# Half of the conditioning blocks of a scan stage computed by GpSimd, VectorE and one matmul instead of eight matmuls

## The chip, the cores and the metric

The kernel runs on one NeuronCore of a Trainium2 chip. TensorE multiplies matrices, VectorE, ScalarE and GpSimd work on rows of 128 partitions, and SyncE issues most of the transfers between HBM and the on-chip memory. The metric is the device time of one execution in microseconds (µs); lower is better. In the rows below PE is TensorE (PEld its weight loads), DVE is VectorE, ACT is ScalarE, POOL is GpSimd and SPq is SyncE's queue.

## The reference, cut to what matters

The model is one layer over 1024 tokens of width 1024. A conditioning vector `c` gives six rows of 1024 numbers; rows 3 and 4 shift and scale the input of the second half of the layer.

```python
sc = jax.nn.silu(c)
mod = (sc @ ada_w[i] + ada_b[i]).reshape(-1, 6, D_MODEL)
x, ctx = mixer_sublayer(x, ctx, mod, ...)            # projection, two-way scan, output projection
x = x + mod[:, 5, None, :] * peer(modulate(rms_norm(x, norm2_w[i]), mod[:, 3], mod[:, 4]), ...)
return rms_norm(x, final_norm_w)
```

## The kernel before, in words

The program is laid out by hand: every engine runs its instructions in the order in which the Python code records them, and an instruction that waits holds up all that stands behind it on the same engine. Of the whole span the change touches the scan of the mixer, from about 353 to 527 µs.

The scan has two loops over blocks of 128 tokens. The first loop (called backward here, `pre` in the code) has twelve turns; the last eight of them carry a state from block 7 down to block 0. A usual turn on TensorE is: transposes (`natural`, L596 and L600), one key product (`key_products`, L361), the carried state's product (`carried`, L644), the new state (`state`, L615) and the decay (`reach`, L634). The state passes through VectorE: `state` ends in L622 and L624, and the next turn's L644 needs the tile `h` that L624 writes. GpSimd scales the tokens (`weigh`, L607, tile `xw`, needed by L615 of the next turn; and L603) and, for the second loop, spreads step sizes over a block (`spread`, L653, tiles `pf` and `pb`, 1024 elements in each partition). The second loop (forward) goes from block 0 to 7; its turn is longer, with sixteen products of `decays` (L698 and L699, which read `pf` and `pb`) and up to four key products.

Beside the scan run two other jobs. `key_products` multiplies a weight with a key in two steps, stores the result (`m_dram<-h2T`, L365) and loads the next pair (L347, L348); after its last store it loads the eight parts of `w_out` into the same tiles (L369). The other job is `modulation`: 24 blocks `ld` of `ada_w`, of 8x128 columns (512 KB) each, loaded into two buffers by `ask` (L294). Blocks 0 to 7 give a gate and are weighted on GpSimd (L316), added up on VectorE (L318 to L321) and summed by a matmul. Blocks 8 to 23 give the columns for shift and scale, each by eight matmuls of one column (L334, fp32, so that each is recorded twice). `beside`, at the end of each turn, lets the generators in `later` go on; `ask` stands just ahead of it and issues loads while fewer than two blocks are in `ready`. After the scan the loop over `later` drains what is left, four small VectorE operations (L337 to L340) form `b2c` and `s2c`, and the output projection begins with `gated(0)` on VectorE (L793).

Of the kernel before, what the change touches and what calls it, by code (L numbers as in the profile page):

```python
# [8 lines left out]
F32 = mybir.dt.float32  # L9
# [5 lines left out]
OP = mybir.AluOpType  # L15
# [3 lines left out]
P = 128  # L19
D = 1024  # L20
KD = D // P
# [51 lines left out]
def layer_kernel(ctx, tc, A, dbg=None):  # L73
    nc = tc.nc
# [10 lines left out]
    ones = glob.tile([P, P], F32, name="ones")  # L85
# [21 lines left out]
    sc = glob.tile([P, KD, 2], F32, name="sc")  # L107
# [27 lines left out]
    lpr = bc_st.enter_context(tc.tile_pool(name="lpr", bufs=2))  # L135
# [132 lines left out]
    queue, later, spare, call = [], [], [0.0], [0]  # L268

    def beside(us):  # L270

        spare[0] += us
        call[0] += 1
        for run in (queue, later):
            for g in list(run):
                while spare[0] > 0:
                    t = next(g, None)
                    if t is None:
                        run.remove(g)
                        break  # L280
                    if t < 0:
                        break
                    spare[0] -= t
        spare[0] = min(spare[0], 0.0)

    ready, since, asked = {}, {}, [0]

    def ask():

        while asked[0] < 24 and len(ready) < 2:  # L290
            j = asked[0]
            ready[j] = lpr.tile([P, KD, P], F32, name="ld")
            since[j] = call[0]
            nc.sync.dma_start(ready[j], ada[:, :, 2048 + j * P:2048 + (j + 1) * P])  # L294
            asked[0] += 1

    def modulation():

        nc.sync.dma_start(gater, A["ada_b"][2048:3072].partition_broadcast(P))
        last = []  # L300

        def spread(j, wa):
            pr = prs[:, j % 4]
            nc.tensor.matmul(pr, ones, wa, start=True, stop=True)
            g = gater[:, j * P:(j + 1) * P]
            nc.vector.tensor_tensor(g, pr, g, op=OP.add)

        prs = psL.tile([P, 4, P], F32, name="pc")
        for j in range(KD):
            while j not in ready:  # L310
                yield -1
            while last and last[0][0] < call[0]:
                spread(*last.pop(0)[1:])
                yield 0.25
            w = ready[j]
            nc.gpsimd.tensor_tensor(w, w, sc[:, :, 0:1].to_broadcast([P, KD, P]), op=OP.mult)  # L316
            yield -1
            nc.vector.tensor_tensor(w[:, :4], w[:, :4], w[:, 4:], op=OP.add)  # L318
            nc.vector.tensor_tensor(w[:, :2], w[:, :2], w[:, 2:4], op=OP.add)
            wa = lpr.tile([P, P], F32, name="wa", bufs=3)  # L320
            nc.vector.tensor_tensor(wa, w[:, 0], w[:, 1], op=OP.add)  # L321
            del ready[j]
            last.append((call[0], j, wa))
            yield 1.1
        yield -1
        while last:
            spread(*last.pop(0)[1:])

        for j in range(KD, 3 * KD):
            while j not in ready or call[0] < since[j] + 2:  # L330
                yield -1
            w = ready.pop(j)
            for k in range(KD):
                nc.tensor.matmul(prs[:, 0, j:j + 1], w[:, k], sc[:, k, 0:1], start=k == 0, stop=k == KD - 1)  # L334
            yield 0.1
        yield -1
        nc.vector.tensor_tensor(b2c, prs[:, 0, KD:2 * KD], adab[:, 24:32], op=OP.add)  # L337
        nc.vector.tensor_tensor(s2c, prs[:, 0, 2 * KD:3 * KD], adab[:, 32:40], op=OP.add)
        nc.vector.tensor_scalar(s2c, s2c, 1.0, None, op0=OP.add)
        nc.vector.tensor_tensor(s2c, s2c, n2c, op=OP.mult)  # L340
        yield 1.0

    def key_products():

        def load(g):
            sk = s2p.tile([P, P], F32, name="sk")
            nc.sync.dma_start(h2T[:, g % KD], A["wqT"][g * P:(g + 1) * P, :])  # L347
            nc.sync.dma_start(sk, A["skT"][g])  # L348
            return h2T[:, g % KD], sk

        nxt = load(0)
        yield
        for g in range(16):
            wq, sk = nxt
            if g + 1 < 16:
                nxt = load(g + 1)
            for k4 in range(2):
                pm = psK.tile([P, 4, P], F32, name="pk")
                for a in range(4):
                    k = k4 * 4 + a  # L360
                    nc.tensor.matmul(pm[:, a], wq[:, k * P:(k + 1) * P], sk, start=True, stop=True)  # L361
                ms = wq.rearrange("p (k n) -> p k n", n=P)[:, k4 * 4:k4 * 4 + 4]
                nc.scalar.activation(ms, pm, AF.Copy)
                if k4:
                    nc.sync.dma_start(m_dram.rearrange("(k p) n -> p k n", p=P)[:, :, g * P:(g + 1) * P],  # L365
                                      wq.rearrange("p (k n) -> p k n", n=P))
                yield
        for k in (4, 5, 6, 7, 0, 1, 2, 3):
            nc.sync.dma_start(h2T[:, k], A["w_out"][k * P:(k + 1) * P, :])  # L369


    with ExitStack() as st:
# [123 lines left out]

        held = {}
        later.append(modulation())
        for n, c in enumerate(order):

# [80 lines left out]
    with ExitStack() as st:  # L581
# [149 lines left out]
        for z in range(NT):  # L731
# [19 lines left out]
            step_keys(1)  # L751
            ask()
            beside(2.2)
        for q in later:
            for _ in q:
                call[0] += 1
                ask()

        for _ in keys:
            pass  # L760
# [483 lines left out]
    with ExitStack() as st:  # L1244
# [85 lines left out]
        more, self_end = [], object()  # L1330
# [300 lines left out]
```

## Time and profile before

| | |
|---|---|
| median of 3 runs | 3053.84 µs (3052.66 to 3054.78) |
| the profiled execution, its own time | 3052.06 µs |
| its span | 3050.3 µs |
| TensorE busy in the span | 93% |
| mean granted TensorE clock | 0.968 |
| TensorE busy from 480 to 500 µs, in the forward loop | 20.00 of 20.00 µs |

The span is what the trace covers; the execution's own time has 1.76 µs around it. The median of the runs lies 1.78 µs over the profiled execution, and sums made in the trace are carried over to the median as differences. The clock is given as a share of full speed: 1.00 is 2.4 GHz and 0.50 is 1.2 GHz.

### The profile page before, as it was taken

The numbers are of one execution on the slowest core, as the hardware profiler recorded it, in microseconds if no ns is written. First come the engines' busy times: TensorE is split into PE (matmuls) and PEld (weight loads), VectorE is DVE, ScalarE is ACT, GpSimd is POOL, SyncE is SP. The second block draws the span as 40 slices with busy tenths as digits, with TensorE's granted clock in tenths as the row PEclk, the third lists the DMA queues.
The fourth block names the chain that finished last, engine by engine and source line by source line (L and its number), as shares of the span: only waits on it lengthen the run. The fifth ranks groups of instructions, "written<-read, shape, count | busy, mean of one in ns | idle before, by whom it ended". The sixth has DMA issues, their size and how long they took to land.

```text
span 3050.3 us, 41960 instructions
## 1 busy us (share of the span) xinstructions
PE 2836.3 (93%) x15129; PEld 2391.2 (78%) x15129; DVE 2570.6 (84%) x5084; ACT 1060.9 (35%) x2026; POOL 1326.0 (43%) x1043
## 2 busy tenths in 40 slices
PE   7999899998888876999999999999999999999996
PEld 3777698764555556898888998998998898998995
DVE  4898756659999999889989998888998888888886
ACT  3224333333667664332222222222222322322222
POOL 0212343420000002666566656566666566666650
PEclk8999899999999987999999999999999999999998
DMA  6211256250221235888889999998998998999993
GB/s 214 61 36 42 86 165 213 77 189 15 118 107 63 111 125 192 308 312 301 311 297 361 324 346 343 326 340 320 337 344 317 334 357 318 336 342 318 328 326 119
DMA packets 334545, 722.68 MB, mean 237 GB/s; under 512 B 24560, under 2 KB 167168, under 8 KB 333056
## 3 DMA queue, kind: packets, MB, share of 16 engines
q0 software_dynamic: 112176, 408.47, 37.1%
q1 hardware_dynamic: 222160, 311.53, 29.5%
q8 instruction: 119, 1.95, 0.2%
q14 instruction: 90, 0.74, 0.1%
HBM read 658.56 MB, written 61.35 MB: 236 GB/s over the span
## 4 chain that ended last, share of the span: by engine, by line
PE 58%; DVE 27%; issue 5%; DMA 5%; POOL 3%; ACT 2%; SPq 0%; DVEq 0%; POOLq 0%; ACTq 0%
PE pa L996 22%; PE pv L1444 8%; PE pv L1445 8%; PE pv L1443 8%; PE pa L68 4%; DVE o L1219 3%; DVE cfm L413 2%; DVE oh L1091 2%; DVE ob L1211 2%; POOL gr L1286 2%; DVE oh L1089 2%; DVE gr L1311 1%; DVE ef L1077 1%; PE pq L953 1%; PE po L68 1%
## 5 line engine op out<-in xcount | busy, mean ns | idle before, releaser
L1286 POOL DMA_INDIRECT gr<-in_peer_v_dram,idx x384 | 546.8, 1424 | 309.3 <-DVE h2T L1323 209.7
L1286 POOL DMA_INDIRECT gr<-in_peer_u_dram,idx x384 | 524.1, 1365 | 361.4 <-DVE gr L1311 249.2
L1444 PE MATMUL pv<-vl,wh 128*128 128x512 f32 x1240 | 495.5, 400 | 19.5 <-DVE vl L61 17.3
L1323 DVE SCALAR_TENSOR_TENSOR h2T<-gr,wv,h2T 128x1024 f32<-128x1024 f32 x381 | 488.5, 1282 | 13.6 <-DMA gr<-in_peer_v_dram,idx 6.0
L1443 PE MATMUL pv<-vh,wl 128*128 128x512 f32 x1240 | 493.4, 398 | 1.5 <-ACT vh L60 1.4
L1445 PE MATMUL pv<-vh,wh 128*128 128x512 f32 x1240 | 493.6, 398 | 0.0
L1311 DVE SCALAR_TENSOR_TENSOR gr<-gr,h2T 128x1024 f32<-128x1024 f32 x384 | 455.5, 1220 | 23.5 <-DMA gr<-in_peer_u_dram,idx 23.3
L60 ACT ACTIVATE vh<-v 128x512 fp32r<-128x512 f32 x256 | 161.5, 632 | 656.1 <-PE pv L1445 616.7
L996 PE MATMUL pa<-hh,ul 128*128 128x320 f32 x2000 | 335.0, 310 | 3.2 <-DVE ul L988 3.2
L996 PE MATMUL pa<-hh,uh 128*128 128x320 f32 x2000 | 334.6, 309 | 0.0
L996 PE MATMUL pa<-hl,uh 128*128 128x320 f32 x2000 | 334.0, 309 | 0.3 <-ACT ga L1406 0.3
L996 PEld LDWEIGHTS pa<-hl,uh 128*128 128x128 f32 x2000 | 304.8, 188 | 3.3 <-ACT ga L1406 0.6
L996 PEld LDWEIGHTS pa<-hh,ul 128*128 128x128 f32 x2000 | 304.2, 188 | 3.7 <-DVE ul L988 3.7
L996 PEld LDWEIGHTS pa<-hh,uh 128*128 128x128 f32 x2000 | 304.4, 188 | 0.0
L1444 PEld LDWEIGHTS pv<-vl,wh 128*128 128x128 f32 x1240 | 235.0, 190 | 80.0 <-DVE vl L61 22.8
L1406 ACT ACTIVATE ga<-pa 128x320 f32<-128x320 f32 x252 | 109.2, 436 | 525.2 <-PE pa L996 507.1
L1443 PEld LDWEIGHTS pv<-vh,wl 128*128 128x128 f32 x1240 | 235.1, 190 | 57.8 <-ACT vh L60 2.4
L61 DVE TENSOR_TENSOR vl<-v,vh 128x512 fp32r<-128x512 f32 x256 | 176.4, 690 | 122.5 <-ACT vh L60 114.9
L1445 PEld LDWEIGHTS pv<-vh,wh 128*128 128x128 f32 x1240 | 235.3, 190 | 56.1
L1197 PEld LDWEIGHTS pg<-o,o 128*128 128x128 f32 x1280 | 174.1, 207 | 128.2 <-ACT o L1214 109.2
L1197 PE MATMUL pg<-o,o 128*128 128x128 f32 x1280 | 188.0, 297 | 75.7 <-ACT o L1214 67.3
L1214 ACT ACTIVATE o<-ob,tr 128x128 f32<-128x128 bf16 x640 | 209.4, 399 | 96.4 <-DVE ob L1211 94.4
(344 smaller groups left out, 4241.5 us busy)
## 6 DMA issues: line engine op xcount, KB each, us to landing
v<-in_peer_v_dram SPq DMA_DIRECT2D x256, 256.0 KB
u<-in_peer_ut_dram SPq DMA_DIRECT2D x87, 512.0 KB
g_dram<-stg SPq DMA_DIRECT2D x10, 4096.0 KB
gm<-g_dram SPq DMA_DIRECT2D x64, 640.0 KB
h2T<-in_peer_ut_dram SPq DMA_DIRECT2D x41, 512.0 KB
ld<-in_ada_w_dram SPq DMA_DIRECT2D x24, 512.0 KB
w<-in_w_in_t_dram SPq DMA_DIRECT2D x21, 512.0 KB
raw<-in_ada_w_dram SPq DMA_DIRECT2D x8, 1024.0 KB
```

Of the source, the lines that this page charges most:

```text
L60: nc.scalar.activation(hi, src, AF.Copy)
L61: (eng or nc.vector).tensor_tensor(lo, src, hi.bitcast(F32), op=OP.subtract)
L68: nc.tensor.matmul(out, a(k)[i], b(k)[j], start=start and t == 0 and k == 0, stop=stop and t == 2 and k == n - 1)
L996: nc.tensor.matmul(pa[half], x[:, k], y[:, k, half * TH:half * TH + TH], start=t == 0 and k == 0, stop=t == 2 and k == KD - 1)
L1197: nc.tensor.matmul(pg[:, j], o2[:, j], o1[:, j], start=True, stop=True)
L1214: nc.scalar.activation(o2[:, j], ob[:, :, j], AF.Copy, scale=tr[:, 1, t4 * 4 + j:t4 * 4 + j + 1])
L1286: nc.gpsimd.indirect_dma_start(out=g, out_offset=None, in_=A[t], in_offset=bass.IndirectOffsetOnAxis(ap=idx[:, b, e:e + 1], axis=0))
L1311: nc.vector.scalar_tensor_tensor(g, g, 1.0, h2, op0=OP.mult, op1=OP.mult, accum_out=act[:, e:e + 1])
L1323: nc.vector.scalar_tensor_tensor(ac, g, wv[:, e:e + 1], ac, op0=OP.mult, op1=OP.add)
L1443: nc.tensor.matmul(Out.pv[t], wl[:, sl], self.vh, start=i == 0, stop=False)
L1444: nc.tensor.matmul(Out.pv[t], wh[:, sl], self.vl, start=False, stop=False)
L1445: nc.tensor.matmul(Out.pv[t], wh[:, sl], self.vh, start=False, stop=i == GE - 1)
```

## The change

Of blocks 8 to 23 the even ones (8, 10, ... 22) still go through eight matmuls. The odd ones (9, 11, ... 23) go to a new generator, `other_columns`: GpSimd multiplies the block by the conditioning vector, VectorE adds its eight slices in three operations, and one matmul with a column of ones sums over the partitions. That matmul is recorded when the next odd block has been given to GpSimd. A block is given to GpSimd as soon as its load has been asked for. The drain after the scan now steps both generators in turn.

```diff
-        for j in range(KD, 3 * KD):
+        later.append(other_columns(prs))
+        for j in range(KD, 3 * KD, 2):
             while j not in ready or call[0] < since[j] + 2:
                 yield -1
             w = ready.pop(j)
             for k in range(KD):
                 nc.tensor.matmul(prs[:, 0, j:j + 1], w[:, k], sc[:, k, 0:1], start=k == 0, stop=k == KD - 1)
             yield 0.1
-        yield -1
+        while len(later) > 1:
+            yield -1
...
+    def other_columns(prs):
+
+        wa = None
+        for j in range(KD + 1, 3 * KD + 2, 2):
+            while j < 3 * KD and j not in ready:
+                yield -1
+            if j < 3 * KD:
+                w = ready[j]
+                nc.gpsimd.tensor_tensor(w, w, sc[:, :, 0:1].to_broadcast([P, KD, P]), op=OP.mult)
+            if wa is not None:
+                nc.tensor.matmul(prs[:, 0, j - 2:j - 1], wa, ones[:, 0:1], start=True, stop=True)
+            yield -1
+            if j < 3 * KD:
+                nc.vector.tensor_tensor(w[:, :4], w[:, :4], w[:, 4:], op=OP.add)
+                nc.vector.tensor_tensor(w[:, :2], w[:, :2], w[:, 2:4], op=OP.add)
+                wa = lpr.tile([P, P], F32, name="wa", bufs=3)
+                nc.vector.tensor_tensor(wa, w[:, 0], w[:, 1], op=OP.add)
+                del ready[j]
+                yield 1.1
...
-        for q in later:
-            for _ in q:
-                call[0] += 1
-                ask()
+        while later:
+            for q in list(later):
+                if next(q, self_end) is self_end:
+                    later.remove(q)
+            call[0] += 1
+            ask()
```

Lines behind the new code stand 22 further down in the changed kernel (24 behind the drain): L361 is L383, L365 is L387, L653 is L675.

The first place is SyncE's queue in the backward loop, before the change: one load of a block (`ld`) to each turn, one of them right behind a store of the key products and one in the turn between.

```order
L365 DMA m_dram<-h2T 128x8x128
L294 DMA ld<-in_ada_w_dram 128x8x128
L347 DMA h2T<-in_wqT_dram 128x1024
L348 DMA sk<-in_skT_dram 128x128
L294 DMA ld<-in_ada_w_dram 128x8x128
L365 DMA m_dram<-h2T 128x8x128
L294 DMA ld<-in_ada_w_dram 128x8x128
```

The same queue with the change, from blocks 11 and 12 on.

```order
L387 DMA m_dram<-h2T 128x8x128
L294 DMA ld<-in_ada_w_dram 128x8x128 x2
L369 DMA h2T<-in_wqT_dram 128x1024
L370 DMA sk<-in_skT_dram 128x128
L387 DMA m_dram<-h2T 128x8x128
L294 DMA ld<-in_ada_w_dram 128x8x128 x2
```

Two loads, the odd block's first, now stand together behind every store, in every other turn; both buffers come free at the end of the turn ahead. In the forward loop they stand together once in two turns.

The second place is TensorE in two turns of the backward loop, before the change: each turn ends in eight matmuls.

```order
L615 MATMUL ps<-xw,bn_2342 128x256 x2
L634 MATMUL psg<-tri,dtx 128x128 x4
L334 MATMUL pc<-sc,ld 128x1 x8
L596 MATMUL pdg<-ident,xsT 128x128 x4
L600 MATMUL pcb<-ident,BT 128x128 x2
L361 MATMUL pk<-sk,h2T 128x128 x4
L644 MATMUL ps<-CT,h_2432 128x128 x4
L615 MATMUL ps<-xw,bn_2401 128x256 x2
L634 MATMUL psg<-tri,dtx 128x128 x4
L334 MATMUL pc<-sc,ld 128x1 x8
```

The same two turns with the change.

```order
L637 MATMUL ps<-xw,bn_2335 128x256 x2
L656 MATMUL psg<-tri,dtx 128x128 x4
L355 MATMUL pc<-ones,wa 128x1
L618 MATMUL pdg<-ident,xsT 128x128 x4
L622 MATMUL pcb<-ident,BT 128x128 x2
L383 MATMUL pk<-sk,h2T 128x128 x4
L666 MATMUL ps<-CT,h_2427 128x128 x4
L637 MATMUL ps<-xw,bn_2396 128x256 x2
L656 MATMUL psg<-tri,dtx 128x128 x4
L335 MATMUL pc<-sc,ld 128x1 x8
```

A turn that ends in one matmul (L355, for the odd block loaded two turns ahead) now alternates with one that ends in eight (L335, for the even block whose load was issued in the turn ahead of it). Until the last store of the key products, thirteen groups of eight become seven groups and five single matmuls.

The third place is GpSimd in the forward loop with the change; before it, the same rows stood there without L353.

```order
L629 TENSOR_TENSOR xw<-xn_2623,wgt 128x512
L675 TENSOR_TENSOR pf<-tri,dt 128x1024
L675 TENSOR_TENSOR pb<-tri,dt 128x1024
L353 TENSOR_TENSOR ld<-ld,sc 128x1024
L629 TENSOR_TENSOR xw<-xn_2564,wgt 128x512
L675 TENSOR_TENSOR pf<-tri,dt 128x1024
L675 TENSOR_TENSOR pb<-tri,dt 128x1024
```

The weighting of the odd block (L353), which waits for that block's load, has come in ahead of the next `xw`, `pf` and `pb`.

## Rows read from the trace of the kernel before

**Rows 1.** The page, its first line.

```profile
span 3050.3 us, 41960 instructions
```

**Rows 2.** Windows: µs, busy time (instructions) of PE, PEld, DVE, ACT, POOL; clock, DMA share, GB/s.

```profile
480.00:500.00 20.00, 20.00 (x185) 19.09 (x184) 13.31 (x14) 7.47 (x12) 11.05 (x6) 1.00 0.66 196
```

**Rows 3.** Chain of waits, backward loop: start, µs, what.

```profile
373.06 0.81 PE pc L304 x2
...
374.25 3.57 PE pc L334 x16
...
384.56 1.68 PE pc L334 x16
...
390.50 1.68 PE pc L334 x16
```

**Rows 4.** Timeline of SyncE's queue: start, µs, what.

```profile
394.45 0.38 SPq L365 DMA_DIRECT2D m_dram<-h2T  x1
...
419.10 0.38 SPq L365 DMA_DIRECT2D m_dram<-h2T  x1
```

**Rows 5.** Chain of waits at the end of the backward loop.

```profile
419.58 5.47 DMA ld<-in_ada_w_dram
...
425.10 1.95 PE pc L334 x16
```

**Rows 6.** Windows of two µs, columns as in rows 2.

```profile
396.00:398.00 2.00, 2.00 (x21) 2.00 (x20) 1.90 (x5) 1.11 (x2) 0.00 (x0) 1.00 0.97 245
...
426.00:428.00 2.00, 2.00 (x16) 2.00 (x16) 0.25 (x1) 0.00 (x0) 0.00 (x0) 0.81 0.71 197
428.00:430.00 2.00, 2.00 (x12) 2.00 (x11) 0.00 (x0) 0.00 (x0) 0.00 (x0) 0.50 0.01 4
430.00:432.00 2.00, 2.00 (x17) 2.00 (x17) 0.00 (x0) 0.00 (x0) 0.00 (x0) 0.84 0.00 0
```

**Rows 7.** Tile `ld`: count, shortest/median/longest ns, first and last start.

```profile
L316 POOL TENSOR_TENSOR ld<-ld,sc x8: 1902/2172/3151, 90.7 to 364.2; 128x1024 f32<-128x1024 f32 x8
L318 DVE TENSOR_TENSOR ld<-ld x8: 678/683/686, 247.1 to 369.6; 128x512 f32<-128x512 f32 x8
L319 DVE TENSOR_TENSOR ld<-ld x8: 424/425/426, 247.9 to 370.3; 128x256 f32<-128x256 f32 x8
L321 DVE TENSOR_TENSOR wa<-ld x8: 291/292/1886, 248.3 to 370.7; 128x128 f32<-128x128 f32 x8
```

**Rows 8.** Timeline from 406 µs, then line L647 in the whole span.

```profile
406.64 1.90 POOL L653 TENSOR_TENSOR pf<-tri,dt 128x1024 f32<-128x1024 f32 x1
408.50 2.35 POOL L653 TENSOR_TENSOR pb<-tri,dt 128x1024 f32<-128x1024 f32 x1
412.23 1.16 PE L644 MATMUL ps<-CT,h 128*128 128x128 f32 x8 [0.63 <-DVE h L624]
L647 DVE TENSOR_TENSOR xsT<-xsT,de x16: 692/693/1622, 383.5 to 526.0; 128x512 f32<-128x512 f32 x16
```

**Rows 9.** Timeline and chain in the forward loop.

```profile
448.77 0.38 SPq L365 DMA_DIRECT2D m_dram<-h2T  x1
454.73 2.94 POOL L653 TENSOR_TENSOR pb<-tri,dt 128x1024 f32<-128x1024 f32 x1 [7.54 <-DVE pf L702]
457.63 1.04 POOL L607 TENSOR_TENSOR xw<-xn,wgt 128x512 f32<-128x512 f32 x1
463.13 0.33 PE psg L698 x2
```

**Rows 10.** Chain of waits at the end of the scan.

```profile
503.19 6.25 DMA h2T<-in_w_out_dram
509.51 11.58 DMA ld<-in_ada_w_dram
521.14 1.95 PE pc L334 x16
...
526.72 0.07 DVE b2c L337
527.19 0.69 DVE xsT L793
```

More of the change, by code (lines that the diff above doesn't have):

```diff
@@ L284, in beside @@
         spare[0] = min(spare[0], 0.0)
-    ready, since, asked = {}, {}, [0]
+    ready, since, asked, self_end = {}, {}, [0], object()
     def ask():
```

## The prediction

> **What bounds the kernel now.** I read the page first for the span [rows 1], then the busy time by windows over the scan, then the chain of waits through it, then SyncE's and GpSimd's timelines beside that chain. The windows say that TensorE has no idle time in the forward loop [rows 2]. The chain says the same of the backward loop: from 384.56 a turn of TensorE follows on the other, and each ends in the eight matmuls of one block, 1.68 µs at full clock [rows 3]. From block to block it is 390.50 − 384.56 = 5.94 µs. So work taken from TensorE shortens the scan, as long as nothing else becomes late. Two things nearly are. At the end of the backward loop the chain runs through a load, which landed at 425.05 for a block that TensorE started at 425.10 [rows 5]. At the end of the scan it runs through the load of the last block, issued at 509.51 and landed at 521.09 behind the loads of `w_out` [rows 10]. The second one matters most: what ends the scan hangs on when the last store of the key products, and the `w_out` loads behind it, get under way.
>
> **What is removed.** Up to that last store thirteen groups of eight matmuls become seven groups and five single matmuls. A group is 1.68 µs [rows 3]; it is sixteen recorded passes, and a single matmul is two of them, so about 0.21 µs. Removed: 6 x 1.68 = 10.1; added: 5 x 0.21 = 1.1. TensorE is ahead by 9.0 µs if it never waits. The three more groups that go after the last store (and their three single matmuls) count for nothing, since the end is not TensorE's there (below).
>
> **What is added beside it.** Eight weightings on GpSimd at 1.90 to 2.17 µs and eight times three additions on VectorE, 0.68 + 0.42 + 0.29 = 1.39 µs [rows 7]. GpSimd was idle for 7.54 µs ahead of one `pb` [rows 9], and VectorE was busy for 13.31 of 20 µs [rows 2]; both have room as a sum. What counts is where these operations wait.
>
> **The waits for the loads.** Before, a block was loaded a whole turn or more ahead of its use. Now both buffers are freed at the end of a long turn, the two loads are issued in the short turn behind the store, and the even block is wanted at the end of the very next turn. The times from a turn's start: the preceding block ends at 390.50 + 1.68 = 392.18, the store is issued at 394.45, so at 2.27 [rows 3, 4]. A short turn is 5.94 − 1.68 + 0.21 = 4.47 long, and in the long turn the group begins at 5.94 − 1.68 = 4.26. The even block is wanted at 4.47 + 4.26 − 2.27 = 6.46 µs after the store's issue. When does it land? The one case with a load right behind a store landed at 425.05 − 419.10 = 5.95 after the store [rows 4, 5]. That is the odd block's time. The even block has 0.52 MB more ahead of its end; where stores and loads of this shape move, 245 GB/s fill 0.97 of the engines [rows 6], so 2.1 µs: 8.1. The lower bound is 6.9, if half of the second load is hidden because the h2T load, which shared those 5.95 µs, now comes behind both. I take 7.5.
>
> The Trainium skill (DMA: Bandwidth & Descriptors, Queues, rings and completion order) says that on each DMA engine the descriptors of one issuer's queue are consumed in ring order, which speaks against the two loads standing together. By it the even block would land at 8.1 and the first pair below would lose 1.6; by my middle value it loses 1.0. The 5.47 µs of the load behind the store agrees with an order, but no row here has two such loads together.
>
> Three pairs are loaded in the backward loop:
> - Blocks 11 and 12: TensorE waits 7.5 − 6.46 = 1.0 (0.4 to 1.6).
> - Blocks 13 and 14: in this short turn GpSimd runs `pf` and `pb`, VectorE is held up and TensorE already waited 0.63 for `h` [rows 8]. The state's way through VectorE does not get shorter, so the 1.47 gained in the turn turns into more of the same wait: a loss of 1.47. Block 14 has landed by then.
> - Blocks 15 and 16: the last turn has no transposes, and TensorE already waited for the load that landed at 425.05. Now that block lands 7.5 − 5.95 = 1.55 later after the store, and TensorE comes 1.47 sooner: 3.0 (2.4 to 3.6).
>
> Together 5.5 (4.3 to 6.5).
>
> The Trainium skill (GPSIMD Engine Reference, Specifications) says that GpSimd shares its SBUF interface with VectorE, in contention with instructions that have two SBUF inputs. The trace agrees: L647, with two such inputs, takes 692 ns and up to 1622 [rows 8]. By it the three additions would be held as well, once for each odd block; by the sum they cost nothing, since VectorE has idle time in which to be held.
>
> **The clock.** After the wait for the block at 425.10 the granted clock falls: 0.81, 0.50 and 0.84 in the three windows from 426 [rows 6], which is 3.1 to 3.4 µs at half speed and 1.6 to 1.7 µs lost. And the group at 374.25, behind a wait that ended at 373.06, took 3.57 instead of 1.68, 1.9 more [rows 3]. Longer waits at blocks 12 and 16 can bring this twice: from 0 to 2 x 3.6 − 1.7 = 5.5 more than now. I take 1.5, near the low end, since one such stretch is in the time already and the wait at block 12 is short.
>
> **GpSimd in the forward loop.** The weighting waits at the head of GpSimd's queue. The odd block lands 5.95 after the store at 448.77, so at 454.7; weighting 2.2, `xw` 1.04, `pf` 1.90, then `pb`, 1.9 to 2.9, which ends at 461.7 to 462.7 instead of 457.67 [rows 8, 9]. Its reader came just behind 463.13 and now comes 1.47 sooner, at about 461.9. So 0 to 0.8 for each such turn, somewhat more if `xw` is late first; two of them lie ahead of the last store: 1.0 (0 to 2.4).
>
> **The end of the scan.** The last block (23) is odd now. Its load still stands behind the eight of `w_out`, but two blocks, not one, stand between the last store and `w_out`: 2.1 later. From its landing the way to L793 was 527.19 − 521.09 = 6.1. Now it is a weighting 1.9, additions 1.39, a matmul and the step to VectorE 0.84 (two matmuls of L304 and their reader, at the same low clock, took that) and 527.19 − 526.72 = 0.47 for `b2c` and `s2c`: 4.6 [rows 3, 7, 10]. Loss 2.1 − 1.5 = 0.6 (0 to 1.0). VectorE's `gated(0)` stands behind these additions, so all of the output projection waits for them; TensorE, ahead by three more groups, just waits longer here. What follows hangs on `gated(0)`, and I let the difference pass to the end.
>
> **Sum.** 9.0 − 5.5 − 1.5 − 1.0 − 0.6 = 0.4 µs saved. The profiled execution, 3052.06, would be 3051.7, and the median 3053.84 would be 3053.4. Best of all bounds: 9.0 − 4.3 = 4.7, 3049.1; worst: 9.0 − 6.5 − 5.5 − 2.4 − 1.0 = −6.4, 3060.2.
>
> **The rivals.**
> - *The loads are in time.* If a pair of loads lands as fast as one does, no block is waited for: the losses at blocks 12 and 16 go, and the 0.4 waited before is gained: 9.0 + 0.4 − 1.5 − 1.0 − 0.6 = 6.3, 3047.5. For it: DMA has pauses between the bursts. Against it: the block at 425.10 was late with one load behind its store. 0.12.
> - *The clock.* Slower, if TensorE runs at 1.2 GHz behind all three even blocks: 3 x 3.6 − 1.7 = 9.1 in place of 1.5, so −7.2, 3061.0. It decides from the point where the wait at block 12 is as long as at block 16, and block 14 is waited for too. For it: the fall at 427 came behind a wait of half a microsecond. Against it: waiting for `h` in that turn leaves block 14 time to land. 0.11. The Trainium skill (TensorE: Matmul & The Clock Gate, The HAM clock gate) says that idle TensorE falls to 1.2 GHz; the rows at 428 agree.
> - *The end follows TensorE.* If block 23 lands ahead of the `w_out` loads' end, the scan ends with TensorE, and the three later groups count, 3 x 1.47 less two more GpSimd waits: 0.4 + 0.6 + 3.4 = 4.4, 3049.4. Against it: the landing at 521.09. 0.07.
>
> **How the numbers follow.** The forecast has 0.70 and its own range is 3049.1 to 3060.2. For 8 in 10 I take 3048.5 to 3060, which leaves out the first rival and most of the second. 0.2%, or 6.1 µs, is about what this measurement can tell from no change. Faster by more: most of the first rival, 0.11. Slower by more: most of the second and the far end of the forecast, 0.11. Within: 0.78.
>
> **What would show it.** In the changed kernel L335 should wait for the `ld` load by about 1 µs at block 12 and about 3 at block 16; at L666 a wait for `h` of some 2 µs behind the backward `pf` and `pb`; L721 short waits for `pb`; at the end L358 a wait for GpSimd, and L817 within a microsecond of where L793 stood. It is wrong if L335 never waits for a load, if the windows show 0.50 behind each even block, or if TensorE is the last to end the scan.

## The result: slower, and most of it behind the last store

The changed kernel took 3071.27 µs (median of 8 runs, 3060.97 to 3079.18) against 3052.43 µs (8 runs) of the kernel before: a ratio of 1.0062, interval 1.0047 to 1.0077, or 18.8 µs more. The forecast was 3053.4 within 3048.5 to 3060.0. In a later group of runs the change cost 14.0 µs (1.0047, 1.0030 to 1.0065). The profiled execution:

```profile
span 3069.3 us, 41781 instructions
```

That is 19.0 µs over [rows 1]. Three marks say where it arose: the first store of the key products in the stretch, the last one, and the first `gated(0)` (L793, now L817).

| mark (µs) | before | changed | difference |
|---|---|---|---|
| store of the first loop | 381.57 | 380.81 | −0.8 |
| last store | 502.12 | 505.37 | +3.3 |
| `gated(0)` | 527.19 | 539.58 | +12.4 |

The scan lost 13.2 µs, of which 9.1 behind the last store, where the prediction had 0.6. Behind `gated(0)` this profile adds 6.6 more, which is not the change's doing for sure (below).

TensorE's waits from 437 to 540 µs (line, what it waited for, µs in total, times, longest). In the kernel before the same query from 430 to 527 µs gives the `pb` wait of 1.7 alone, so that one is not the change's.

```profile
PE pk L383 <- DMA sk<-in_skT_dram: 3.8, 2, 2.1
PE pc L355 <- DVE wa L361: 3.0, 1, 3.0
PE ps L637 <- POOL xw L629: 2.4, 1, 2.4
PE psg L721 <- POOL pb L675: 1.7, 1, 1.7
PE ps L666 <- DVE h L646: 1.6, 1, 1.6
PE pdg L742 <- DVE xsT L744: 1.4, 1, 1.4
```

The chain of waits through the backward loop (start, µs, what) answers to [rows 3, 5]: TensorE now waits for two even blocks, 12 and 16, where it waited for one.

```profile
394.10 5.45 DMA ld<-in_ada_w_dram
399.59 1.95 PE pc L335 x16
...
418.47 7.09 DMA ld<-in_ada_w_dram
425.60 3.24 PE pc L335 x16
```

From its store's issue (391.71 and 417.36) the even block landed after 7.8 and 8.2 µs. The forecast was 7.5. The prediction's estimate by the ring order that the Trainium skill states (DMA: Bandwidth & Descriptors, Queues, rings and completion order) was 8.1, which is nearer. But the block's own load took 5.45 and 7.09, so at block 12 a good part of the delay lay ahead of its issue: the size agrees, the order of the two loads isn't shown by it. TensorE's own wait was 1.5 µs at block 12 and 3.8 at block 16. The second group runs at half clock, 3.24 in place of 1.68.

SyncE's queue in the forward loop (answers to [rows 9]) shows a wait that the prediction had no price for. Behind the store stand two blocks, then the key pair:

```profile
450.91 0.38 SPq L387 DMA_DIRECT2D m_dram<-h2T  x1
451.34 2.32 SPq L294 DMA_DIRECT2D ld<-in_ada_w_dram  x2
453.70 1.51 SPq L369 DMA_DIRECT2D h2T<-in_wqT_dram  x1
455.30 0.38 SPq L370 DMA_DIRECT2D sk<-in_skT_dram  x1
```

`sk` goes out 4.39 µs after the store, before it was 451.29 − 448.77 = 2.52, and it has two blocks ahead of it. In the chain of waits it ends 5.50 µs later, and the next key product starts at 460.94.

The end of the scan, in the chain of waits (answers to [rows 10]):

```profile
505.84 5.40 DMA ld<-in_ada_w_dram
...
513.24 1.05 POOL xw L629
514.33 1.71 PE ps L637 x4
...
526.94 2.75 DVE em L725
...
536.97 0.69 DVE ld L358
537.69 0.44 DVE ld L359
538.14 0.30 DVE wa L361
538.49 0.50 PE pc L355 x2
```

Block 21's load ends at 511.24. GpSimd, which has had its weighting at the head of the queue since the turn before, does that first (1.90) and then `xw`, for which TensorE stands still. The clock behind that wait stands in the windows (behind the length of the window PE's busy time, clock third from the end; answers to [rows 6]):

```profile
512.00:514.00 2.00, 0.00 (x0) 0.00 (x0) 1.97 (x4) 0.22 (x1) 2.00 (x2) 1.00 1.03 382
514.00:516.00 2.00, 1.67 (x6) 1.38 (x6) 2.00 (x2) 0.00 (x0) 2.00 (x2) 0.69 1.03 412
516.00:518.00 2.00, 2.00 (x12) 2.00 (x11) 1.90 (x3) 0.00 (x0) 2.00 (x2) 0.50 1.02 408
...
524.00:526.00 2.00, 2.00 (x15) 1.98 (x14) 0.39 (x1) 0.24 (x1) 0.00 (x0) 0.75 0.10 27
```

Two µs without a matmul, then 1.2 GHz until 525: at 0.69, four windows of 0.50 and 0.75 that is 2 x 0.31 + 4 x 1.0 + 2 x 0.25 = 5.1 µs lost. The changed kernel's second profile has the same wait and the same loss again. That the wait brought the fall is argued, not shown (see the last section). Then L725 takes 2.75 µs, while GpSimd weights block 23 from 526.14 on; the other seven take 1.23. And the three additions of block 23 stand last on VectorE, with one matmul behind them.

VectorE's last turn divides the 9.1 µs. First the kernel before, then the changed one:

```profile
516.51 1.23 DVE L702 TENSOR_TENSOR pf<-pf,pb 128x1024 f32<-128x1024 f32 x1 [2.55 <-PE psg L698]
526.03 0.69 DVE L647 TENSOR_TENSOR xsT<-xsT,de 128x512 f32<-128x512 f32 x1
```

```profile
525.61 1.23 DVE L724 TENSOR_TENSOR pf<-pf,pb 128x1024 f32<-128x1024 f32 x1 [4.67 <-PE psg L720]
536.36 0.69 DVE L669 TENSOR_TENSOR xsT<-xsT,de 128x512 f32<-128x512 f32 x1
526.14 2.46 POOL L353 TENSOR_TENSOR ld<-ld,sc 128x1024 f32<-128x1024 f32 x1 [5.81 <-DMA ld<-in_ada_w_dram]
```

From the last store to the turn's first operation it is 20.24 µs instead of 14.39: 5.85 come with TensorE. From there to L669 it is 10.75 instead of 9.52, 1.23 more, and from L669 to `gated(0)` 3.22 instead of 1.16, 2.06 more, for the additions and the matmul.

### The profile page after: what moved, and what is told of

It reads as the page before. It is cut to its first block, busy times and chain, and to the rows that moved or that the text cites. A ratio compares the mean times of both kernels' runs of the same rounds, so it can differ in the third digit from the quotient of the medians.

```text
span 3069.3 us, 41781 instructions
## 1 busy us (share of the span) xinstructions
PE 2837.7 (92%) x15017; PEld 2389.9 (78%) x15017; DVE 2601.1 (85%) x5108; ACT 1059.1 (35%) x2026; POOL 1347.8 (44%) x1051
## 3 DMA queue, kind: packets, MB, share of 16 engines
q8 instruction: 118, 1.93, 0.2%
## 4 chain that ended last, share of the span: by engine, by line
PE 58%; DVE 27%; DMA 6%; issue 5%; POOL 3%; ACT 2%; SPq 0%; DVEq 0%; POOLq 0%; ACTq 0%
PE pa L1020 22%; PE pv L1468 8%; PE pv L1469 8%; PE pv L1467 8%; PE pa L68 4%; DVE o L1243 3%; DVE cfm L435 2%; PE po L68 2%; DVE oh L1115 2%; DVE ob L1235 2%; DVE oh L1113 2%; DMA gr<-in_peer_u_dram,idx 2%; DVE gr L1335 1%; POOL gr L1310 1%; DVE ef L1101 1%
## 5 line engine op out<-in xcount | busy, mean ns | idle before, releaser
L1468 PE MATMUL pv<-vl,wh 128*128 128x512 f32 x1240 | 495.5, 400 | 20.8 <-DVE vl L61 20.6
```

Source lines behind the costliest of these rows:

```text
L1468: nc.tensor.matmul(Out.pv[t], wh[:, sl], self.vl, start=False, stop=False)
```

## The experiments

Ratios are to runs of the kernel before on the same chip. All marks are of one profile each, start of the last store and of `gated(0)`.

| kernel | last store | `gated(0)` | ratio of the times (interval) |
|---|---|---|---|
| before / again | 502.12 / 501.41 | 527.19 / 528.03 | 1 |
| changed / again | 505.37 / 506.07 | 539.58 / 540.46 | 1.0062 / 1.0047 |
| b_odd1 | 500.58 | 523.80 | 1.0004 (0.9990 to 1.0019) |
| b_odd1_buf3 | 496.88 | 528.53 | 1.0000 (0.9987 to 1.0012) |
| b_odd1_buf3c | 497.15 | 520.37 | 0.9985 (0.9973 to 0.9998) |
| a_keys2 | 505.16 | 536.85 | 1.0048 (1.0029 to 1.0067) |
| a_tiny | 504.16 | 533.02 | 1.0030 (1.0019 to 1.0040) |
| b_tail | 497.94 | 529.61 | 1.0029 (1.0018 to 1.0040) |
| a_tail8 | 504.03 | 531.88 | 1.0037 (1.0023 to 1.0051) |
| a_bwd8 | 503.20 | 533.98 | 1.0037 (1.0023 to 1.0052) |
| a_fwd8 | 512.35 | 540.09 | 1.0035 (1.0019 to 1.0050) |
| a_buf3 | 527.37 | 548.03 | 1.0085 (1.0053 to 1.0117) |
| a_buf3_late | 520.18 | 545.41 | 1.0063 (1.0041 to 1.0086) |
| a_buf3b | 500.63 | 529.17 | 1.0012 (0.9999 to 1.0025) |
| a_best4 | 495.53 | 524.90 | 1.0000 (0.9988 to 1.0013) |
| a_best4c | 496.99 | 522.00 | 0.9989 (0.9978 to 0.9999) |

**The TensorE part alone** (b_odd1, in the kernel before):

```diff
-            for k in range(KD):
+            n = 1 if j % 2 else KD
+            for k in range(n):
```

> The kernel before, in which every odd block from 9 on is given one matmul instead of eight (seven eighths of its sum are left out); nothing is put on GpSimd or VectorE and the loads keep their order. It is the TensorE part of the change without its price. Theory 'waits': TensorE bounds the scan and what the change lost lies in waits for loads and for GpSimd. Then six groups up to the last store of the key products save 6 x 1.47 = 8.8 us, that store comes 8 to 9 us earlier than in the kernel before, and the time is about 3044. Rival 'not the bound': the scan hangs on the loads or on the state's way through VectorE, TensorE just waits longer elsewhere: store within 2 us of before, time 3050 to 3053.

The time did not move, and the last store came 1.5 µs earlier, not 8.8. In the forward loop the two groups saved 1.6 and 1.1 µs of a turn. The backward loop gave back more than it had saved, with no weighting and no pairs of loads: from store to store its first two intervals became 1.4 and 1.2 µs shorter, the last two 1.7 and 1.9 longer. TensorE's waits from 385 to 437 µs:

```profile
PE ps L645 <- DVE h L625: 2.4, 2, 2.2
PE pc L335 <- DMA ld<-in_ada_w_dram: 2.0, 1, 2.0
```

The group behind the load (block 16) took 3.58 µs, at half clock, and the clock was at 0.66 and 0.50 in the four µs from 410, behind the wait for `h`, too. So block 16's turn had no slack left. Before, TensorE was ready for that block at 424.66 (it waited 0.44), 5.08 µs behind the issue at 419.58, and the load takes 5.47 [rows 5], or 5.94 in this profile. The turn ahead of it hangs on `h`. Block 12, begun 6.0 µs behind its issue here, came without a wait.

**The same with loads a turn earlier** (b_odd1_buf3c; a third buffer, in slot 7 of `h2T`):

```diff
-            while j not in ready or call[0] < since[j] + 2:
+            while j not in ready or call[0] < since[j] + 3:
...
+            elif j == KD + 1:
+                ready[j] = h2T[:, 7].rearrange("p (k n) -> p k n", n=P)
```

A first form had `w_out` loaded over a block that TensorE had still to read (that block's columns came from `w_out`): TensorE waited 4.4 µs for `w_out`, and `gated(0)` moved to 528.53.

> The kernel before with every odd block from 9 on given one matmul instead of eight (seven eighths of its sum are left out), and besides a third buffer (slot 7 of h2T; the key products use the other seven), so that each block is loaded two turns ahead of its use and all ahead of w_out. Theory 'load time' (in the backward loop a load takes as long as a turn, so that a shorter turn only waits for it): with the loads a turn earlier the 8.8 us taken from TensorE show; the last store comes 6 to 9 us earlier than in the kernel before, against 1.5 us with two buffers, and gated(0) as much. Rival 'state' (the way of the state through VectorE and GpSimd sets the backward loop): the last store within 3 us of that with two buffers.

> As the kernel before with one matmul for each odd block and a third buffer, but with the last two blocks out of the slot that w_out takes. Theory 'load time': last store at about 497 as there, and now the way to gated(0) is 25 us or less, so gated(0) at 519 to 522 against 527.2 of the kernel before, and the time 5 to 8 us under it. Rival 'taken back': gated(0) as early, but the time within 3 us of the kernel before, because the output projection runs longer (its clock) by what the scan gained. Rival 'state': gated(0) not before 525.

Now no group waits for a load. The last store came 5.0 µs earlier, `gated(0)` 6.8, and the time fell by 4.9. Both the load and the state limit the backward loop. It is 5.0 and not 8.8 since the wait for `h` behind `pf` and `pb` was still there (1.6 longer than before), the clock in the four µs behind it was low (1.7 lost), and a key product waited 1.0 for `sk`; the wait of 0.4 for block 16 went. 8.8 − 1.6 − 1.7 − 1.0 + 0.4 = 4.9.

```profile
410.00:412.00 2.00, 2.00 (x10) 1.63 (x9) 1.27 (x2) 0.00 (x0) 0.41 (x1) 0.63 1.04 282
412.00:414.00 2.00, 2.00 (x12) 2.00 (x11) 1.40 (x3) 0.14 (x1) 0.00 (x0) 0.52 0.01 3
```

**Key pairs two ahead** (a_keys2, in the changed kernel):

```diff
-        nxt = load(0)
+        nxt = [load(0), load(1)]
...
-            if g + 1 < 16:
-                nxt = load(g + 1)
+            if g + 2 < 16:
+                nxt.append(load(g + 2))
```

> The changed kernel with the key products' pairs loaded two ahead instead of one, so that no key product waits for a pair that stands behind two blocks in SyncE's queue. Theory 'loads': the two waits of 1.7 and 2.1 us for sk in the forward loop go, the last store comes 3 to 4 us earlier than in the changed kernel, but the wait for xw at the end of the scan and the low clock behind it stay: about 3067. Rival 'GpSimd queue': pb and xw are late by as much, since the weighting still waits for its load: the waits move to L637 and L721, and the time stays at 3070 to 3072.

The wait for `sk` went, and the last store stayed (505.16), though in an execution whose first store came 1.6 µs later (382.36). In the last such turn the chain of waits now goes through GpSimd, from the landing of the odd block to TensorE:

```profile
484.90 1.90 POOL ld L353
486.81 1.45 POOL xw L629
488.25 2.30 POOL pf L675
490.55 2.31 POOL pb L675
492.91 0.49 PE psg L721 x2
```

The time (1.0048) can't be told from the changed kernel's (1.0062 and 1.0047), and the waits moved as the rival said: 1.7 µs for `xw` and 0.6 for `pb` from 430 to 505 µs. The wait for `sk` and GpSimd's queue lay beside each other: with the first gone, 2.3 of its 3.8 µs came back through the second. The forward loop gained the rest, 1.4 (438.59 to 505.16, 66.6 µs against 68.0).

**Short operations, same waits** (a_tiny, in the changed kernel):

```diff
-                nc.gpsimd.tensor_tensor(w, w, sc[:, :, 0:1].to_broadcast([P, KD, P]), op=OP.mult)
+                nc.gpsimd.tensor_tensor(w[:, :, :8], w[:, :, :8], sc[:, :, 0:1].to_broadcast([P, KD, 8]), op=OP.mult)
```

and the three additions likewise.

> The changed kernel with the weighting and the three additions of an odd block cut to 8 of 128 columns (the rest of its sum is left out); every load, every wait and the order stay. Theory 'waits': still 12 to 19 us over the kernel before. Rival 'work' (the length of the operations on GpSimd, and what they hold back on VectorE): within 6 us of the kernel before.

Between the two, 8.7 µs over the kernel before. The last store is 1.2 µs earlier than in the changed kernel, `gated(0)` 6.6. So the length of the operations is more than half of what the end of the scan lost (the way from the last store to `gated(0)` is 28.9 µs, against 34.2 in the changed kernel and 25.1 before); what comes up to the last store is mostly there without it.

**The end alone, and all but the end.** b_tail gives only 21 and 23 to GpSimd, a_tail8 only 9 to 19:

```diff
-        for j in range(KD, 3 * KD, 2):
+        for j in list(range(8, 21)) + [22]:
```

```diff
-        for j in range(KD, 3 * KD, 2):
+        for j in list(range(8, 21, 2)) + [21, 22, 23]:
```

> The kernel before, in which blocks 21 and 23 alone go to GpSimd, all others through eight matmuls, one to a turn. Theory 'end of the scan': up to the last store nothing changes (within 1 us), and the way from it to gated(0) grows from 25 to 30 us or more: 5 to 9 us over the kernel before. Rival: the last store's loads are the cause and not the weighting; with loads one to a turn the way stays within 2 us of 25.

> The changed kernel up to block 20; 21, 22 and 23 go through eight matmuls, and the loads of 22 and 23 stand behind w_out. Theory 'end of the scan' (of the changed kernel's 12 us at gated(0), 9 come up behind the last store: the weighting of 21 ahead of the last xw, the half clock behind that wait, the weighting and additions of 23): the way from the last store to gated(0) falls from 34 to 25 to 28 us, and the time to 6 to 12 us over the kernel before. Rival: the way stays over 31 us, as the two late loads or the clock take its place.

b_tail's way from the last store to `gated(0)` was 31.7 µs against 25.1 and 26.6 of the two profiles of before, with two waits of the same length, although its loads go out one to a turn:

```profile
PE ps L638 <- POOL xw L630: 2.4, 1, 2.4
PE pc L356 <- DVE wa L362: 2.2, 1, 2.2
```

They are not the same waits, though. b_tail's wait for `xw` stands in the last turn, behind the weighting of block 23, which waits for its load; in the changed kernel it stands a turn earlier, behind that of block 21.

```profile
516.83 1.90 POOL L354 TENSOR_TENSOR ld<-ld,sc 128x1024 f32<-128x1024 f32 x1 [9.56 <-DMA ld<-in_ada_w_dram]
518.69 1.04 POOL L630 TENSOR_TENSOR xw<-xn,wgt 128x512 f32<-128x512 f32 x1
```

So b_tail shows what a weighting ahead of `xw` costs there, and a_tail8 what these two blocks cost in the changed kernel. b_tail's way also holds a wait of 1.2 for `pb` behind block 21's weighting, and 1.7 of low clock from 508 to 514, ahead of the two waits (last section).

In a_tail8 the way was 27.9 µs against the changed kernel's 34.2, with a wait of 2.4 for block 19's additions in it. So two blocks out of eight make most of the loss at the end. Of the time they are less: a_tail8 is still 11.2 µs over the kernel before. b_tail's `gated(0)` is only 2.4 µs later than before all the same, since its backward loop, with the instructions of before, was 2.9 µs shorter in this execution (no half clock at its end) and began 1.3 µs earlier. Of the 10.4 µs by which it was slower, 5 to 6.6 lie on this way; the others stay without a place.

**One loop each** (a_bwd8 gives 17, 19, 21 and 23 to GpSimd, a_fwd8 gives 9, 11, 13 and 15):

```diff
-        for j in range(KD, 3 * KD, 2):
+        for j in list(range(8, 17)) + [18, 20, 22]:
```

```diff
-        for j in range(KD, 3 * KD, 2):
+        for j in [8, 10, 12, 14] + list(range(16, 24)):
```

> Blocks 8 to 16 go through eight matmuls, one block to a turn as before; of the later ones the odd ones 17, 19, 21 and 23 go to GpSimd. Theory 'end of the scan': the backward loop is that of the kernel before, the two forward turns gain 1 us each at most, and the last turn waits for xw behind the weighting of 21 with the clock at half behind it: 7 to 11 us over the kernel before. Rival 'backward loop': within 4 us of the kernel before.

> Of the odd blocks only 9, 11, 13 and 15 (backward loop) go to GpSimd; 16 to 23 go through eight matmuls, one block to a turn. The loads of 22 and 23 both stand behind w_out, which costs about 1 to 2 us by itself. Theory 'end of the scan' (the weighting of block 21 ahead of the last xw, and the additions of 23, cost most): only the backward loop's loss of 3 us and those 2 us are left, about 5 us over the kernel before. Rival 'backward loop' (late even blocks and the clock there, passed on to the end): 12 us or more over it.

Each half cost some 11 µs, together more than the whole change, so the halves don't add up. For a_bwd8 that is what the theory gave, though its wait for `xw` (1.8) stands behind the weighting of 23, as in b_tail, and not of 21. For a_fwd8 it is near the rival's: its backward loop, the same instructions as the changed kernel's, took 3.7 µs more from the first store to the forward loop's first. The waits for blocks 12 and 14 were 1.2 and 0.3 longer, and the low clock behind block 16 lasted longer (0.57 over the 12 µs from 428, against 0.57 over the 8 µs from 426 there). A wait of 2.5 µs for an odd block's additions followed in the forward loop.

**A third buffer in the changed kernel** (a_buf3, a_buf3_late, then a_buf3b):

```diff
-        while asked[0] < 24 and len(ready) < 2:
+        while asked[0] < 24 and len(ready) < (3 if 24 > asked[0] >= KD else 2):
...
-            while j < 3 * KD and j not in ready:
+            while j < 3 * KD and (j not in ready or call[0] < since[j] + 2):
...
             if wa is not None:
+                while call[0] <= done:
+                    yield -1
```

a_buf3 has the first piece, a_buf3_late two, a_buf3b all.

> The changed kernel with a third buffer for the blocks (slot 7 of h2T; the key products use the other seven), so that loads are issued about one to a turn, and all of them ahead of the w_out loads. The weighting still stands right behind the issue of its load. Theory 'loads' (two loads together are late, and the key pair behind them): no group of eight and no key product waits for a load, the last store comes about 9 us before that of the kernel before, 3043 to 3048. Theory 'GpSimd queue' (the weighting, which waits some 5 us for its load at the head of GpSimd's queue, holds back xw, pf and pb): L637 and L721 wait 1 to 3 us in each turn with an odd block, and the time stays over 3058.

> As the third-buffer kernel, but the weighting of an odd block is put off by a turn, as an even block's matmuls are, so that GpSimd doesn't wait for the load. Theory 'loads' alone: same time as the third buffer without that, within 2 us. Theory 'GpSimd queue': faster than it by 5 us or more, 3043 to 3048. If neither the loads nor GpSimd's queue cost the time (the three additions on VectorE, or the clock by itself), both third-buffer kernels stay at 3060 or more.

> The changed kernel with a third buffer for the blocks (slot 7 of h2T; the key products use the other seven), an odd block weighted a turn after its load is issued, and its matmul recorded a turn behind its additions. Loads go out one to a turn and all ahead of w_out; nothing on GpSimd or TensorE should then stand behind a load. It does the same arithmetic as the changed kernel. Theory 'waits' (the change loses by waits for loads, in TensorE's and in GpSimd's queue): faster than the kernel before by 2 to 8 us. Rival 'work' (GpSimd's and VectorE's added operations themselves hold the state's way through VectorE): it stays 5 to 15 us over the kernel before.

The first two were as slow as the changed kernel or slower, by a side effect: the next odd block came so early that an odd block's matmul stood directly behind its own additions. TensorE in a_buf3 from 430 to 505 µs:

```profile
PE pc L364 <- DVE wa L370: 13.1, 3, 6.2
```

They say nothing of loads, only what a matmul costs behind a chain through two other engines. a_buf3b has the change's arithmetic without these waits: the loss shrinks to 2.7 µs, with an interval that just takes in no change. The forecast gain did not come, and two waits are left that name where: TensorE waits 3.0 µs for the additions of 23 at the end of the scan, and 4.5 for the first `pb` of the forward loop (1.7 before), which stands on GpSimd behind 15's weighting.

**A version without the waits** (a_best4c; in a_best4 `w_out` again overwrote a block ahead of its use). One generator; 9, 11, 17 and 19 go to GpSimd two turns behind their load's issue, additions and matmul a turn later each, all others through eight matmuls; four buffers.

```diff
+            if pm:
+                nc.tensor.matmul(prs[:, 0, pm[0]:pm[0] + 1], pm[1], ones[:, 0:1], start=True, stop=True)
...
+            if j in (9, 11, 17, 19):
+                pa, w = j, ready[j]
+                nc.gpsimd.tensor_tensor(w, w, sc[:, :, 0:1].to_broadcast([P, KD, P]), op=OP.mult)
```

> A version meant to keep the gain without the waits, of the same arithmetic: blocks 9, 11, 17 and 19 go to GpSimd a turn or more behind their loads, their additions and their matmul a turn later each, all others through eight matmuls; four buffers (two of them slots of h2T), so that loads stand one to two turns ahead and all ahead of w_out. If the waits named so far are the whole loss: last store 4 to 6 us earlier than in the kernel before, time 2 to 6 us under it. If GpSimd's operations themselves hold back the scan: 0 to 5 us over it.

> The version meant to keep the gain (blocks 9, 11, 17, 19 on GpSimd, four buffers, loads one to two turns ahead), with the last two blocks out of the slots that w_out takes; same arithmetic as the changed kernel. Half of the TensorE saving, 4 groups: last store about 496, gated(0) at 521 to 524. If the time follows: 3 to 6 us under the kernel before. If the stages behind take it back: within 3 us of it.

3050.55 against 3054.43 µs of the kernel before on the same chip: 3.9 µs less, with an interval that ends at 0.9999, so barely told from no change. `gated(0)` came 5.2 µs earlier. From 437 to 522 µs TensorE has one wait left:

```profile
PE pk L390 <- DMA sk<-in_skT_dram: 0.8, 1, 0.8
```

Not all of that is the matmuls': in this execution the clock stayed at 1.00 through the backward loop, whose end lost 1.7 in the profile of before [rows 6]. And no run has the earlier loads with all groups left on TensorE, so what GpSimd's share is worth beside the earlier loads is not shown.

**Both kernels again.**

> The changed kernel itself again, on the same chip as the others of this group: 12 to 19 us over the kernel before. Its profile tells which of its waits come again: those for the even blocks 12 and 16, for sk twice, for xw at the end, each within 1 us of the first profile; the low clock behind them may differ by some us.

> The kernel before itself again, for its profile: the waits as in the first one; the low clock at the end of the backward loop may be missing, which would put the later stores up to 3 us earlier, and gated(0) at 524 to 528.

Every store and `gated(0)` of the two profiles of a kernel lie within 1.0 µs of each other, and the waits came again. The low clock at the end of the backward loop was there again, so that guess was wrong. But the spans of the two profiles of before are 3050.3 and 3059.1 µs, and all but 0.8 of the 8.8 µs arise behind `gated(0)`. From there to the end the profiles of all kernels take 2522.5 to 2537.3 µs, and the changed kernel's two lie inside (2529.7 and 2526.0). So the 6.6 µs that its first profile adds there are no more than what one kernel shows against itself; whether the change has a share in them stays open.

## Why the prediction was wrong, step by step

- *TensorE saves 9.0 µs up to the last store if it never waits.* The removal was sized rightly (1.47 a group; the forward turns of b_odd1 show it), but "a block was loaded a whole turn or more ahead of its use" was read as slack, and block 16 was issued only 5.08 µs before TensorE was ready for it, less than its load takes. b_odd1 kept 1.5 of 8.8 µs without any cost of the change. The sum does charge the two turns where the rest went, 14 and 16, but with 1.5 each, and b_odd1 has a stretch of low clock in both.
- *The waits for the loads, 5.5, and the clock, 1.5.* By the intervals from store to store, with 1.47 a turn added: at block 12 2.5 lost (forecast 1.0), at 14 1.4 (1.5, right), at 16 5.3 (3.0). Together 9.2 against 7.0; places and order were right, the landing was 0.3 to 0.7 later than my value, and the clock fell behind both waits. (The upper ends, 1.6, 1.47 and 3.6, add up to 6.7 and not to 6.5.)
- *GpSimd in the forward loop, 1.0.* From 437.37 to 505.37 is 68.0 µs against 66.9, with 2.9 saved: 4.1 lost. The waits were not for `pb` but for `sk`. I had moved that load behind two blocks to reckon when the blocks land, and did not ask who waits for it. a_keys2 shows `pb` next in line.
- *The end of the scan: "the three more groups … count for nothing, since the end is not TensorE's there", a loss of 0.6.* This is the step that failed most: it was 9.1. The term had two parts. The load of block 23 was to come 2.1 later behind the last store. GpSimd began on it 20.8 µs behind the store, where it had landed after 19.0: 1.8 later, but by luck. SyncE issued it at 519.28 only, when block 22's late matmuls had freed its buffer, and not just behind `w_out`:

```profile
SPq L294 <- PE pc L335: 3.8, 1, 3.8
```

The way from there to `gated(0)` was to be 4.6 instead of 6.1, and it was 13.4. The sum let the additions follow the weighting, but they stand on VectorE behind the last turn: the weighting ended at 528.60, the additions began at 536.97, and L358 did not wait for GpSimd. And that turn hangs on TensorE, which before had waited for block 23's load hardly at all (busy for 1.93 of the 2.00 µs around the landing at 521.09 [rows 10]):

```profile
520.00:522.00 2.00, 1.93 (x13) 1.47 (x12) 1.97 (x4) 0.00 (x0) 0.00 (x0) 1.00 0.02 6
```

So a TensorE that comes later ends later. I left the last turns out of the count, with their savings also their GpSimd waits: 2.4 µs for `xw`, 5.1 of low clock behind them, the longer L725, and the additions of 23. a_tail8 shows that the two blocks make 6.4 of the 9.1, a_tiny that the operations' length is more than half of it.
- *The rivals.* "The end follows TensorE" named the right place with the wrong sign. "The clock" had the right sign: half clock came behind 12 and 16 as it said, not behind 14, and behind `xw`, where it did not look. The rows at 428, which it says agree, have TensorE busy all the time, behind a wait of 0.44. The range ended at 3060.0 since no term had a bound for the last turns.
- *VectorE held by GpSimd costs nothing.* L725 at 2.75 instead of 1.23 µs stands on the chain, and at the end there was no idle time to hide it. The Trainium skill (GPSIMD Engine Reference, Specifications) says that GpSimd's SBUF interfaces are shared with VectorE, in contention with instructions that have two SBUF inputs. L725 has two, so the trace agrees.

## What to carry to other kernels

Before work is taken from the busiest engine, ask how long the next thing that it needs has been under way: where a load takes as long as the time from its issue to its use, as block 16's did, a shorter turn only waits. An operation that waits for a load belongs on an in-order queue where that load has landed, so move its issue a turn earlier first and the work second (a_best4c against the change). And count the last turns of a loop by themselves: what is late there is late in the next stage.

## What the runs showed of the hardware that was not expected

VectorE's additions of a block took 0.68 and 0.42 µs alone and up to 2.37 and 2.00 beside GpSimd's operations (L358 and L359 at 425.89 and 466.01), so an operation that is off the path by its own length can be on it by its neighbour's.

The same instructions got different clocks in different executions: the low clock behind block 16 lasted 10 µs in a_fwd8, behind a wait of 3.4, and 6.8 in the changed kernel, behind one of 3.8. Nor is a fall tied to a wait. In the last forward turns of b_tail TensorE was busy without a gap from 500 to 514, and the granted clock fell all the same:

```profile
506.00:508.00 2.00, 2.00 (x18) 1.92 (x16) 2.00 (x3) 0.04 (x1) 1.27 (x1) 1.00 1.02 412
508.00:510.00 2.00, 2.00 (x16) 2.00 (x16) 1.86 (x4) 0.00 (x0) 0.00 (x0) 0.77 1.04 416
510.00:512.00 2.00, 2.00 (x11) 2.00 (x11) 0.16 (x1) 0.00 (x0) 0.00 (x0) 0.50 1.02 404
512.00:514.00 2.00, 2.00 (x18) 2.00 (x17) 0.13 (x1) 0.00 (x0) 0.00 (x0) 0.87 1.04 364
```

In a_best4c a wait of 1.7 µs for `h`, up to 398.63, was followed by no fall (1.00 in every window to 432). What sets the clock at such places stays open. One kernel's time spread by 5 to 18 µs over its runs, up to as much as the change cost.
